# A hybrid attention and expert layer: the end of the output projection taken two outputs at a time, transposes on both sides of a broadcast, and small work moved between VectorE and GpSimd

## The chip, the cores and the metric

The kernel runs on one core of one Trainium2 chip. The metric is the device time of one execution in microseconds (us), the median of several executions. Beside it stands one profiled execution, whose span (first to last instruction on the core) is a little shorter than its own time. Engines are named as the profile names them: PE (TensorE matmuls), PEld (its weight loads), DVE (VectorE), ACT (ScalarE), POOL (GpSimd) and SP, which issues most transfers.

## The reference

One decoder layer on 256 tokens of width 1024, in float32, cut to what matters here:

```
mod = silu(c) @ w_ada + b_ada                 # split into sh1, sc1, g1, sh2, sc2, g2
h   = rmsnorm(x, norm1_g) * (1 + sc1) + sh1
q, k, v, u = split(h @ w_in)                  # 512 columns each
mixed = concat(attention(q, k, v), pooling(u)) @ w_out
x   = x + g1 * mixed
h2  = rmsnorm(x, norm2_g) * (1 + sc2) + sh2
s   = scores of (h2 @ peer_wq) against two sets of 128 sub-keys, top 16 of each, top 16 of the sums
x   = x + g2 * sum over chosen experts e of gate_e * gelu(peer_u[e] . h2) * peer_v[e]
out = rmsnorm(x, final_g)
```

There are 16384 experts. The kernel does not gather the chosen ones; it multiplies by all of `peer_u` and `peer_v`, with gates that are zero for experts that were not chosen.

## The kernel before, in words

The whole kernel is one program written out by hand: each engine runs its instructions in the order in which the code issues them, and waits where data or a buffer is missing. Activations lie transposed (channels on partitions, 256 tokens along the free axis). Large matmuls run on numbers split in two: `hi` is the rounded part (ACT copies it), `lo` the rest (DVE subtracts, L522), and three products hi*hi, hi*lo and lo*hi are summed in PSUM.

The stages, in order of time:

- **Start.** `x`, `c` and a table `band` are loaded. `score_bias(h)` makes the bias table of each of 8 heads from `band`: heads 0 to 4 by one DVE instruction each (L192), heads 5 to 7 by two POOL instructions each (L194, L195). DVE and ACT square `x` (L254, L256), DVE adds the squares up (L259), PE sums them over partitions (L262), and `rstd_rows` makes 1/rms: a square root on ACT, four small DVE instructions, two diagonal tiles `dg` (L230), and a matmul of `ones` with `dg` (L231) that spreads the row over all partitions. `keep_warm(n)` (L241) issues n matmuls of `ones` whose result nobody reads.
- **First projection** (L330, L335), eight blocks `k` of `w_in`. In each, DVE makes two columns of `mod` (`ada_step`, L201, a dot product of a `w_ada` block with silu(c)), the scaled rows `t` (L306), two `lo` tiles (L316) and `hl` (L318); ACT makes `hh` (L313) and two `whi` (L274).
- **Attention and pooling**, with `ada_steps` between: these columns (G1, then SC2 and SH2 by turns) are needed later. Then the **output projection** `out_proj(n)`: block n of `w_out` (L457), eight outputs `m` each, for n = 0 to 7 as the heads' results come.
- **Second norm.** After all of block 7, DVE adds the projection to `x` (L545), ACT squares (L548), PE sums (L550), then 16 transposes (`turn_rows`, L536) of the new `x`, which ACT copies to `x2nat` (`turn_back`, L540), then `rstd_rows` again, and the loop over `k` that makes `t` (L591), `h2h` (L592) and `h2l` (L606) and multiplies them with the first three tiles of `peer_wq` (`first`, L584).
- **Queries, then `peer_u`** (L567, L568, L571), 16 and 128 tiles; the first 16 write to the PSUM banks of `q_bank` and are copied out by ACT (L839).
- **`peer_v`** (L992), steps i = 0 to 127, twelve matmuls each. Tiles come through three `raw` buffers that SP fills in order. The last three tiles are taken early, at steps 40, 50 and 60. In this stage the last columns of `mod`, g2, are made too: for each block k a load by POOL (`tail_load`), a DVE dot product (`tail_dot`, L201) and a diagonal tile (L951), a matmul of `ones` with it (`tail_pe`, L956), and a copy by ACT (`tail_evac`, L961), so that g2 stands in a row on all partitions. The final norm follows.

Loads are queued in `Loads`: SP issues them strictly in the order in which they were added, each when a buffer of its kind is free (7 of kind `ada`, 8 of `big`, 3 of `raw`).

Of the kernel before, what the change touches and what calls it, by code (L numbers as in the profile page):

```python
# [87 lines left out]
def _body(ctx, tc, xT, c, w_ada, cols, w_in, pool_w, w_out, peer_wq, subkeys, peer_u, peer_v, final_g,  # L88
# [84 lines left out]
    early = {40 + 10 * j: NQ + 2 * NK - 3 + j for j in range(3)}  # L173
    order = list(range(NQ + 2 * NK - 3))
    for i, n in early.items():
        order.insert(order.index(NQ + NK + i + 1) + 1, n)
# [364 lines left out]

    for m in range(0, KD, 2):
        out_proj(7, (m, m + 1))
    for m in range(KD):
# [2 lines left out]
        sqk = prepb.tile([P, T], F32, name="t", bufs=4)
        nc.scalar.activation(sqk, x2[:, m, :], AF.Square)  # L548
        for tb in range(2):
            nc.tensor.matmul(ps2[:, tb:tb + 1], lhsT=sqk[:, tb * P:(tb + 1) * P], rhs=ones[:, 0:1],  # L550
                             start=(m == 0 and tb == 0), stop=(m == KD - 1), skip_group_check=True)
# [599 lines left out]
```

## Time and profile before

| | |
|---|---|
| median of 3 runs | 922.27 us (920.63 to 922.82) |
| the profiled execution's own time | 922.48 us |
| its span | 920.7 us |
| PE busy | 906.1 us, 98% of the span |
| DVE busy | 692.5 us, 75% |
| ACT busy | 456.0 us, 50% |
| POOL busy | 15.1 us, 2% |
| moved by DMA | 185.40 MB, mean 201 GB/s |

The profiled execution lies 0.2 us over the median. PE has work nearly all the time, so what a change can win is PE work that goes away, PE waits, and PE work that runs at a lower clock. Time at which PE has nothing to do lies before the first projection, around the second norm, and after the last matmul.

### The profile page before, as it was taken

What the parts mean: (1) busy time and instruction counts of PE and PEld (TensorE: products, weight loads), DVE (VectorE), ACT (ScalarE), POOL (GpSimd) and SP (SyncE); (2) the same over time, 40 slices, a digit from 0 to 9 for tenths busy, and PEclk for the clock granted to TensorE, in tenths of its full rate; (3) what the DMA queues carried; (4) which work ended last, traced back from release to release, by engine and by line L of the source; (5) the groups of instructions that cost most, each with busy time, mean ns of one, the idle gap of its engine ahead of it and who ended that gap; (6) DMA issues with size and microseconds to landing.
All of it is one profiled execution on the core that took longest, in us unless ns stands there. A gap on an engine that the chain in (4) does not pass through costs nothing.

```text
span 920.7 us, 15894 instructions
## 1 busy us (share of the span) xinstructions
PE 906.1 (98%) x6267; PEld 829.4 (90%) x6267; DVE 692.5 (75%) x1285; ACT 456.0 (50%) x656; POOL 15.1 (2%) x24
## 2 busy tenths in 40 slices
PE   8999999999999999999999999999999999999996
PEld 7987889999999999999999998888888888888885
DVE  7999769899989778888889866555556656666665
ACT  5456355545454555454444445444456554444542
POOL 3000000000000000000000000000000000000001
PEclk9999999999999999999999999999999999999999
DMA  9988644566555555545555555666776776666551
GB/s 342 408 326 298 262 131 152 158 186 190 194 184 184 161 165 169 172 161 164 171 167 165 161 179 184 191 198 190 222 246 219 249 231 220 210 213 219 185 180 47
DMA packets 52061, 185.40 MB, mean 201 GB/s; under 512 B 6033, under 2 KB 6545, under 8 KB 51986
## 3 DMA queue, kind: packets, MB, share of 16 engines
q1 hardware_dynamic: 50402, 179.12, 58.8%
q0 software_dynamic: 1440, 5.25, 1.9%
q8 instruction: 49, 0.80, 0.4%
q14 instruction: 26, 0.21, 0.1%
q10 hardware_dynamic: 144, 0.01, 0.0%
HBM read 183.31 MB, written 1.05 MB: 200 GB/s over the span
## 4 chain that ended last, share of the span: by engine, by line
PE 96%; DVE 2%; ACT 1%; DMA 1%; issue 0%; SPq 0%; DVEq 0%
PE psum L992 37%; PE psum L567 15%; PE psum L568 14%; PE psum L571 14%; PE psum L330 4%; PE psum L457 3%; PE psum L798 2%; PE psum L799 2%; PE psum L335 1%; PE psum L584 1%; PE psum L848 1%; DMA xt<-in_xT_dram 1%; PE psum L241 0%; PE psum L550 0%; PE psum L536 0%; DVE a L1033 0%
## 5 line engine op out<-in xcount | busy, mean ns | idle before, releaser
L522 DVE TENSOR_TENSOR lo<-raw,hi 128x1024 fp32r<-128x1024 f32 x269 | 328.6, 1223 | 201.3 <-ACT hi L517 194.6
L517 ACT ACTIVATE hi<-raw 128x1024 fp32r<-128x1024 f32 x269 | 285.2, 1060 | 314.0 <-PE psum L992 142.0
L567 PE MATMUL psum<-h,hi 128*128 128x256 f32 x1128 | 273.4, 283 | 0.4 <-ACT q L839 0.4
L568 PE MATMUL psum<-h,hi 128*128 128x256 f32 x1128 | 269.7, 280 | 0.0
L992 PE MATMUL psum<-hi,h 128*128 128x512 f32 x972 | 240.8, 389 | 0.0
L992 PEld LDWEIGHTS psum<-hi,h 128*128 128x128 f32 x972 | 181.6, 188 | 37.3 <-ACT hi L517 0.2
L567 PEld LDWEIGHTS psum<-h,hi 128*128 128x128 f32 x1128 | 213.1, 189 | 0.6 <-ACT q L839 0.6
L568 PEld LDWEIGHTS psum<-h,hi 128*128 128x128 f32 x1128 | 213.0, 189 | 0.0
L571 PE MATMUL psum<-h,lo 128*128 128x256 f32 x1128 | 154.5, 280 | 0.0
L571 PEld LDWEIGHTS psum<-h,lo 128*128 128x128 f32 x1128 | 141.7, 189 | 0.0
L992 PE MATMUL psum<-lo,h 128*128 128x512 f32 x486 | 130.3, 388 | 0.0
L992 PEld LDWEIGHTS psum<-lo,h 128*128 128x128 f32 x486 | 91.2, 188 | 18.8
L201 DVE SCALAR_TENSOR_TENSOR junk<-ada,silc 128x1025 f32<-128x1025 f32 x40 | 48.9, 1221 | 0.9 <-DMA ada<-in_w_ada_dram 0.6
L817 ACT ACTIVATE a<-psum 128x256 f32<-128x256 f32 (+22 forms) x54 | 16.7, 352 | 60.6 <-DVE a L814 57.9
L899 DVE TENSOR_TENSOR h<-a,h 128x1024 fp32r<-128x1024 f32 x31 | 37.8, 1218 | 0.0
L798 PE MATMUL psum<-ah,ohb 128*128 128x128 f16 x256 | 33.1, 220 | 0.0
L799 PE MATMUL psum<-al,ohb 128*128 128x128 f16 x256 | 32.7, 218 | 0.0
L895 ACT ACTIVATE h<-a 128x1024 fp32r<-128x1024 f32 x31 | 32.4, 1046 | 0.0
L457 PE MATMUL psum<-cat,big 128*128 128x256 f32 x128 | 28.9, 382 | 0.0
L457 PEld LDWEIGHTS psum<-cat,big 128*128 128x128 f32 x128 | 23.9, 190 | 3.9 <-issue 0.7
L814 DVE SCALAR_TENSOR_TENSOR a<-psum,a 128x768 f32<-128x768 f32 (+31 forms) x42 | 27.2, 667 | 0.0
L825 ACT ACTIVATE a<-psum 128x512 f32<-128x512 f32 (+30 forms) x59 | 26.4, 448 | 0.0
(221 smaller groups left out, 755.5 us busy)
## 6 DMA issues: line engine op xcount, KB each, us to landing
raw<-in_peer_u_dram SPq DMA_DIRECT2D x128, 512.0 KB, 3.6
raw<-in_peer_v_dram SPq DMA_DIRECT2D x128, 512.0 KB, 4.3
ada<-in_w_ada_dram SPq DMA_DIRECT2D x40, 512.5 KB, 8.2
big<-in_w_in_dram SPq DMA_DIRECT2D x16, 512.0 KB, 10.3
raw<-in_peer_wq_dram SPq DMA_DIRECT2D x16, 512.0 KB, 3.7
a<-in_w_ada_dram POOLq DMA_DIRECT2D x8, 512.5 KB, 5.3
big<-in_w_out_dram SPq DMA_DIRECT2D x8, 512.0 KB, 6.9
out_dram<-a SPq DMA_DIRECT2D x4, 256.0 KB, 2.2
```

What stands on the lines that cost most here:

```text
L201: nc.vector.scalar_tensor_tensor(jk, blk, 1.0, sil, op0=ALU.mult, op1=ALU.mult, accum_out=ada[:, v * 8 + k:v * 8 + k + 1])
L330: nc.tensor.matmul(banks[m // 2][:, m % 2, :], lhsT=a[:, cs], rhs=b, start=(st and n == 0 and m % 2 == 0), stop=(sp and n == 2), skip_grou ...
L457: nc.tensor.matmul(ob[m // 2][:, m % 2, :], lhsT=w[:, m * P:(m + 1) * P], rhs=cat[:, k, :], start=(n == 0 and m % 2 == 0), stop=(n == 7), ...
L517: nc.scalar.activation(hi, raw, AF.Copy)
L522: nc.vector.tensor_sub(lo, raw, hi.bitcast(F32))
L567: nc.tensor.matmul(o, lhsT=hi[:, cs], rhs=h2h[:, k, :], start=(k == 0), stop=False, skip_group_check=True)
L568: nc.tensor.matmul(o, lhsT=hi[:, cs], rhs=h2l[:, k, :], start=False, stop=False, skip_group_check=True)
L571: nc.tensor.matmul(o, lhsT=lo[:, cs], rhs=h2h[:, k, :], start=False, stop=(k == KD - 1), skip_group_check=True)
L798: nc.tensor.matmul(o[:, t, :], lhsT=b[:, pr, :, e], rhs=ah[:, pr, :, e], start=True, stop=False)
L799: nc.tensor.matmul(o[:, t, :], lhsT=b[:, pr, :, e], rhs=al[:, pr, :, e], start=False, stop=True)
L899: nc.vector.tensor_sub(lo, a, hi.bitcast(F32))
L992: nc.tensor.matmul(ycols(tb, cs) if o is None else o, lhsT=a[:, i % 4, tb * P:(tb + 1) * P], rhs=b[:, cs], start=st, stop=sp, skip_group_c ...
```

## The change

The parts, each with what it does:

- **Output projection.** Blocks 6 and 7 of `w_out` are taken together, two outputs at a time. After each pair, `x2_pair` updates two rows of `x` and squares them; the `sums` of a pair are issued one pair later, between matmuls of the projection. One `ada_step` (SC2 of block 7) moves between the second and the third pair, the last one (SH2 of block 7) from ahead of `rstd_rows` to behind it.
- **Transposes.** Eight go ahead of the matmul that spreads 1/rms, eight behind it.
- **Loads.** Three `w_out` blocks are queued ahead of all eight G1 blocks of `w_ada`, six of which stood ahead of them.
- **Start.** All score biases are made by DVE: heads 0 to 5 at the start, 6 and 7 in blocks 3 and 4 of the first projection. POOL makes none. The warm-up matmuls around `rstd_rows` become 4 and 3 (5 and 5 before). The formula of 1/rms changes, with as many instructions as before.
- **`q_bank`** goes through four PSUM banks, three before.
- **`peer_v` stage.** The last three tiles are loaded by POOL to a place of their own, at steps 14, 18 and 22, and split at steps 30, 34 and 38. The g2 columns are made every 7 steps (9 before); a DMA writes each column into a row on one partition, and at step 108 one POOL instruction, `partition_broadcast`, copies the row to all partitions. The eight diagonal tiles, matmuls and copies go.

```diff
@@
-    for k, n in zip((4, 5, 6, 7, 0, 1, 2, 3, None), (6, 0, 0, 2, 2, 2, 2, 2, 8)):
+    for k, n in zip((4, 5, 6, 7, 0, 1, 2, 3, None), (0, 0, 0, 8, 2, 2, 2, 2, 8)):
         for _ in range(n):
             ada_load(*next(todo))
         if k is not None:
             load("big", ("wo", k), prep, [P, D], w_out[k], 8)
...
-    def score_bias(h):
-        b = biast[:, h, P:384]
-        if h < 5:
-            nc.vector.scalar_tensor_tensor(b, bandt[:, 0, :], -slopes[h], bandt[:, 1, :], op0=ALU.mult, op1=ALU.subtract)
-        else:
-            nc.gpsimd.tensor_scalar(b, bandt[:, 0, :], -slopes[h], None, op0=ALU.mult)
-            nc.gpsimd.tensor_sub(b, b, bandt[:, 1, :])
+    def score_bias(hs):
+        for h in hs:
+            nc.vector.scalar_tensor_tensor(biast[:, h, P:384], bandt[:, 0, :], -slopes[h], bandt[:, 1, :],
+                                           op0=ALU.mult, op1=ALU.subtract)
...
-    keep_warm(5)
+    keep_warm(4)
     rstd_rows(banks[7][:, 0, 0:2], banks[6][:, 0, :])
-    keep_warm(5)
+    keep_warm(3)
...
     for k in range(KD):
+        if k in (3, 4):
+            score_bias(range(k + 3, k + 4))
...
-    for n in range(4, 7):
+    for n in range(4, 6):
         ada_steps(3)
         out_proj(n)
-    ada_steps(2)
+    ada_steps(4)
...
+    def x2_pair(m):
+        for n in (m, m + 1):
+            nc.vector.scalar_tensor_tensor(x2[:, n, :], ob[n // 2][:, n % 2, :], acol(G1, n), xt[:, n, :],
+                                           op0=ALU.mult, op1=ALU.add)
+            SQ[n] = prepb.tile([P, T], F32, name="t", bufs=4)
+            nc.scalar.activation(SQ[n], x2[:, n, :], AF.Square)
+
+    def sums(m):
+        for n in (m, m + 1):
+            for tb in range(2):
+                nc.tensor.matmul(ps2[:, tb:tb + 1], lhsT=SQ[n][:, tb * P:(tb + 1) * P], rhs=ones[:, 0:1],
+                                 start=(n == 0 and tb == 0), stop=(n == KD - 1), skip_group_check=True)
+
     for m in range(0, KD, 2):
-        out_proj(7, (m, m + 1))
-    for m in range(KD):
-        nc.vector.scalar_tensor_tensor(x2[:, m, :], ob[m // 2][:, m % 2, :], acol(G1, m), xt[:, m, :],
-                                       op0=ALU.mult, op1=ALU.add)
...
-        if m == 3:
-            split_hi(0, [prepb.tile([P, D], F32R, name=x, bufs=2) for x in ("hi", "lo")])
-    turn_rows(range(KD))
+        for n in (6, 7):
+            out_proj(n, (m, m + 1))
+        x2_pair(m)
+        if m >= 2:
+            sums(m - 2)
+        if m == 2:
+            ada_steps(1)
+        if m == 4:
+            split_hi(0, two())
+    sums(KD - 2)
     split_lo(0)
-    ada_steps(1)
+    turn_rows(range(4))
     rstd_rows(ps2[:, 0:2], psb)
+    turn_rows(range(4, KD))
     turn_back(0)
     turn_back(2)
-    split_hi(1, [prepb.tile([P, D], F32R, name=x, bufs=2) for x in ("hi", "lo")])
+    split_hi(1, two())
+    ada_steps(1)
...
-        return psum[:, 1 + n % 3, 0:T]
+        return psum[:, (1 + n) % 4, 0:T]
...
-        jk = f1_[:, 0:D + 1]
-        ada_dot(G2, k, blk_of(k), jk, silc2)
-        nc.vector.tensor_scalar(jk[:, 0:P], ident, acol(G2, k), None, op0=ALU.mult)
-
-    def tail_pe(k):
-        o = psum[:, 6 + k % 2, :]
-        TP[k] = o
-        nc.tensor.matmul(o[:, 0:P], lhsT=ones, rhs=f1_[:, 0:P], start=True, stop=True)
...
+    def tail_row(k):
+        nc.gpsimd.dma_start(g2row[:, k * P:(k + 1) * P], acol(G2, k))
+
+    def tail_spread():
+        nc.gpsimd.partition_broadcast(g2r, g2row)
+
+    def early_load(j):
+        ld.ready["raw", NQ + 2 * NK - 3 + j] = early_raw[j]
+        nc.gpsimd.dma_start(early_raw[j], peer_v[NK - 3 + j])
...
```

Where the instructions stand is read from the built programs. First PE around the second norm, before the change: `big_941` is the last block of `w_out`, `t_...` are the squares of one output each, `xt_77` is the new `x`, and `dg_1129` the diagonal tile of 1/rms.

```order
L457 MATMUL psum_134<-cat_743,big_941 128x256 x8
L550 MATMUL psum_134<-ones_67,t_1060 128x1 x2
L550 MATMUL psum_134<-ones_67,t_1065 128x1 x2
L550 MATMUL psum_134<-ones_67,t_1070 128x1 x2
L550 MATMUL psum_134<-ones_67,t_1075 128x1 x2
L550 MATMUL psum_134<-ones_67,t_1083 128x1 x2
L550 MATMUL psum_134<-ones_67,t_1088 128x1 x2
L550 MATMUL psum_134<-ones_67,t_1093 128x1 x2
L550 MATMUL psum_134<-ones_67,t_1098 128x1 x2
L536 MATMUL psum_134<-ident_66,xt_77 128x128 x16
L231 MATMUL psum_134<-dg_1129,ones_67 128x256
L584 MATMUL psum_134<-h2_71,hi_1079 128x256
```

The same place after it, from the sums of the second pair on (`big_921` and `big_935` are blocks 6 and 7 of `w_out`; L450 is the projection, L529 the transposes, L223 the matmul with `dg`):

```order
L550 MATMUL psum_134<-ones_67,t_1050 128x1 x2
L550 MATMUL psum_134<-ones_67,t_1053 128x1 x2
L450 MATMUL psum_134<-cat_737,big_921 128x256 x2
L450 MATMUL psum_134<-cat_737,big_935 128x256 x2
L550 MATMUL psum_134<-ones_67,t_1066 128x1 x2
L550 MATMUL psum_134<-ones_67,t_1069 128x1 x2
L550 MATMUL psum_134<-ones_67,t_1083 128x1 x2
L550 MATMUL psum_134<-ones_67,t_1086 128x1 x2
L529 MATMUL psum_134<-ident_66,xt_77 128x128 x8
L223 MATMUL psum_134<-dg_1114,ones_67 128x256
L529 MATMUL psum_134<-ident_66,xt_77 128x128 x8
L595 MATMUL psum_134<-h2_71,hi_1075 128x256
```

Eight of the sums stand behind the last of the projection now, sixteen before, and eight of the transposes have moved behind the matmul with `dg`.

Then DVE at the same place, before the change (`lo` is `split_lo(0)`; the dot products of L201 read SC2 and SH2 of block 7, `ada_1011` and `ada_1014`; `m` to `dg` is `rstd_rows`; the last row makes `t` of k = 0):

```order
L201 SCALAR_TENSOR_TENSOR junk_76,ada_64<-ada_1011,silc_75 128x1025
L212 SCALAR_TENSOR_TENSOR ada_64<-ada_64,colt_63 128x1
L545 SCALAR_TENSOR_TENSOR xt_77<-psum_134,ada_64,xt_77 128x256 x8
L522 TENSOR_TENSOR lo_1080<-raw_1016,hi_1079 128x1024
L201 SCALAR_TENSOR_TENSOR junk_76,ada_64<-ada_1014,silc_75 128x1025
L226 TENSOR_SCALAR m_1122<-psum_134 128x2
L218 RECIPROCAL m_1122<-m_1122 128x2
L219 SCALAR_TENSOR_TENSOR m_1122<-m_1122 128x2
L220 TENSOR_TENSOR m_1122<-m_1122 128x2
L221 SCALAR_TENSOR_TENSOR m_1122<-m_1122 128x2
L230 TENSOR_SCALAR dg_1129<-ident_66,m_1122 128x128 x2
L591 SCALAR_TENSOR_TENSOR t_1138<-xt_77,ada_64,psum_134 128x256
```

And after it, from the point behind the first four updates of `x`:

```order
L196 SCALAR_TENSOR_TENSOR junk_76,ada_64<-ada_1005,silc_75 128x1025
L207 SCALAR_TENSOR_TENSOR ada_64<-ada_64,colt_63 128x1
L542 SCALAR_TENSOR_TENSOR xt_77<-psum_134,ada_64,xt_77 128x256 x4
L515 TENSOR_TENSOR lo_1076<-raw_1010,hi_1075 128x1024
L213 TENSOR_SCALAR m_1107<-psum_134 128x2
L216 RECIPROCAL m_1107<-m_1107 128x2
L217 TENSOR_TENSOR m_1107<-m_1107,m_1107 128x2
L218 TENSOR_TENSOR m_1107<-m_1107 128x2
L219 RECIPROCAL m_1107<-m_1107 128x2
L222 TENSOR_SCALAR dg_1114<-ident_66,m_1107 128x128 x2
L196 SCALAR_TENSOR_TENSOR junk_76,ada_64<-ada_1008,silc_75 128x1025
L602 SCALAR_TENSOR_TENSOR t_1132<-xt_77,ada_64,psum_134 128x256
```

The dot product of SH2 has moved from ahead of `m` to between `dg` and `t`, and `lo` now follows the last updates of `x` with only `m` behind it.

Last POOL's queue, from the start's work on, before the change (`a0` is the large buffer whose first parts fall free in the `peer_v` stage):

```order
L195 TENSOR_TENSOR biast_78<-biast_78,bandt_79 128x256
L964 DMA a0_1264<-in_c_dram 128x1024
L946 DMA a0_1264<-in_w_ada_dram 128x1025 x3
L974 DMA a0_1264<-in_final_g_dram 128x1024
L946 DMA a0_1264<-in_w_ada_dram 128x1025 x5
L1045 TENSOR_TENSOR a0_1264<-a0_1264 128x512 x2
```

And its end after the change, from the load of the last g2 block on (L965 writes a column into the row, the second ISA row is the broadcast):

```order
L956 DMA a0_1258<-in_w_ada_dram 128x1025
L965 DMA a0_1258<-ada_64 1x128x1
L968 ISA
L968 ISA a0_1258<-a0_1258 128x1024
L1067 ISA
L1067 TENSOR_TENSOR a0_1258<-a0_1258 128x512 x2
```

POOL has no arithmetic at the start any more; it has small transfers and one broadcast in the `peer_v` stage instead.

## Rows read from the trace of the kernel before

**Rows 1.** The page's chain of work that ended last: shares of the span.

```profile
PE 96%; DVE 2%; ACT 1%; DMA 1%; issue 0%; SPq 0%; DVEq 0%
```

**Rows 2.** Waits of PE: who waited for whom, us in total, times, longest.

```profile
PE psum L262 <- DVE x2nat L259: 1.7, 1, 1.7
```

**Rows 3.** Timeline of DVE and POOL: start us, us, instruction, count.

```profile
7.41 1.22 DVE L254 TENSOR_TENSOR x2nat<-xt 128x512 f32<-128x512 f32 x1
8.55 3.27 DVE L259 TENSOR_TENSOR x2nat<-x2nat 128x256 f32<-128x256 f32 x6
62.56 0.68 DVE L379 TENSOR_TENSOR pool<-x2nat 128x504 f32<-128x504 f32 x1
...
6.86 1.22 POOL L195 TENSOR_TENSOR biast<-biast,bandt 128x256 f32<-128x256 f32 x1
9.42 0.78 POOL L195 TENSOR_TENSOR biast<-biast,bandt 128x256 f32<-128x256 f32 x1
```

**Rows 4.** The chain in order of time, start and first projection: start us, us.

```profile
16.12 2.13 PE psum L241 x10
18.25 1.62 PE psum L330 x12
...
41.09 1.42 PE psum L330 x12
```

**Rows 5.** Timeline of ACT, DVE and SP, first projection; idle before in brackets.

```profile
16.67 0.51 ACT L313 ACTIVATE hh<-t,ada 128x256 fp32r<-128x256 f32 x1 [1.31 <-DVE t L306]
38.94 0.51 ACT L313 ACTIVATE hh<-t,ada 128x256 fp32r<-128x256 f32 x1 [3.13 <-DVE t L306]
...
58.06 1.22 DVE L201 SCALAR_TENSOR_TENSOR junk<-ada,silc 128x1025 f32<-128x1025 f32 x1
60.16 1.22 DVE L379 TENSOR_TENSOR x2nat<-uT 128x1020 f32<-128x1020 f32 x1 [0.88 <-ACT uT L348]
...
43.78 10.31 SPq L122 DMA_DIRECT2D ada<-in_w_ada_dram  x6
```

**Rows 6.** One window, first projection: busy of PE, PEld, DVE, ACT, POOL; PEclk, DMA, GB/s.

```profile
18.50:58.00 39.50, 39.50 (x294) 37.63 (x294) 39.26 (x64) 17.66 (x23) 0.00 (x0) 1.00 1.03 404
```

**Rows 7.** The chain in order of time, second norm.

```profile
107.38 3.46 PE psum L550 x32
110.85 3.46 PE psum L536 x16
...
117.38 10.11 PE psum L584 x68
```

**Rows 8.** Timeline of DVE and ACT, second norm.

```profile
104.83 3.46 DVE L545 SCALAR_TENSOR_TENSOR xt<-psum,ada,xt 128x256 f32<-128x256 f32 x8 [1.93 <-PE psum L457]
110.88 0.16 DVE L226 TENSOR_SCALAR m<-psum 128x2 f32<-128x2 f32 x1 [0.31 <-PE psum L550]
112.10 0.48 DVE L230 TENSOR_SCALAR dg<-ident,m 128x128 f32<-128x128 f32 x2
114.78 0.48 DVE L591 SCALAR_TENSOR_TENSOR t<-xt,ada,psum 128x256 f32<-128x256 f32 x1 [2.20 <-PE psum L231]
...
115.30 0.51 ACT L592 ACTIVATE h<-t,ada 128x256 fp32r<-128x256 f32 x1 [1.06 <-DVE t L591]
```

**Rows 9.** Windows of 1 us, second norm (columns as in rows 6).

```profile
118.00:119.00 1.00, 1.00 (x5) 0.74 (x4) 1.00 (x3) 0.69 (x2) 0.00 (x0) 0.50 0.85 320
121.00:122.00 1.00, 1.00 (x10) 1.00 (x10) 1.00 (x4) 0.72 (x2) 0.00 (x0) 1.00 0.27 111
```

**Rows 10.** Timeline of PE: the fourth query tile begins.

```profile
127.95 0.38 PE L567 MATMUL psum<-h,hi 128*128 128x256 f32 x1 [0.36 <-ACT q L839]
```

**Rows 11.** The chain in order of time, `peer_v` stage: one of eight such pieces.

```profile
742.34 0.22 PE psum L956 x2
```

**Rows 12.** Timeline of DVE and PE, `peer_v` stage.

```profile
833.31 1.23 DVE L522 TENSOR_TENSOR lo<-raw,hi 128x1024 fp32r<-128x1024 f32 x1 [1.49 <-ACT hi L517]
...
834.74 1.07 PE L992 MATMUL psum<-lo,h 128*128 128x512 f32 x4
```

More of the change, by code (lines that the diff above doesn't have):

```diff
@@ L172, in _body @@
     LAST = 5
[L173 to L176, printed above, removed]
+    early = {30 + 4 * j: NQ + 2 * NK - 3 + j for j in range(3)}
+    order = range(NQ + 2 * NK - 3)
     for n in order:
@@ L226, in rstd_rows @@
         nc.vector.tensor_scalar(m[:, 0:2], ps, 1.0 / D, EPS, op0=ALU.mult, op1=ALU.add)
-        rsqrt(m[:, 2:4], m[:, 0:2], m[:, 4:6])
+        nc.scalar.activation(m[:, 2:4], m[:, 0:2], AF.Sqrt)
+        nc.vector.reciprocal(m[:, 4:6], m[:, 2:4])
+        nc.vector.tensor_mul(m[:, 4:6], m[:, 4:6], m[:, 0:2])
+        nc.vector.tensor_add(m[:, 4:6], m[:, 4:6], m[:, 2:4])
+        nc.vector.reciprocal(m[:, 2:4], m[:, 4:6])
         dg = prep.tile([P, 2, P], F32, name="dg", bufs=1)
         for tb in range(2):
-            nc.vector.tensor_scalar(dg[:, tb, :], ident, m[:, 2 + tb:3 + tb], None, op0=ALU.mult)
+            nc.vector.tensor_scalar(dg[:, tb, :], ident, m[:, 2 + tb:3 + tb], 2.0, op0=ALU.mult, op1=ALU.mult)
         nc.tensor.matmul(psb, lhsT=ones, rhs=dg.rearrange("p a t -> p (a t)"), start=True, stop=True)
@@ L249, in _body @@
     keep_warm(5)
-    for h in range(NH):
-        score_bias(h)
+    score_bias(range(0, 6))
     for n, (a, b) in enumerate(xch):
@@ L540, in turn_back, with two @@
         nc.scalar.activation(x2nat[:, :, m * P:(m + 2) * P], turned[m // 2].rearrange("p (a d) -> p a d", a=2), AF.Copy)
-    for m in range(0, KD, 2):
-        out_proj(7, (m, m + 1))
-    for m in range(KD):
-        nc.vector.scalar_tensor_tensor(x2[:, m, :], ob[m // 2][:, m % 2, :], acol(G1, m), xt[:, m, :],
-                                       op0=ALU.mult, op1=ALU.add)
[L547 to L551, printed above, removed]
-        if m == 3:
-            split_hi(0, [prepb.tile([P, D], F32R, name=x, bufs=2) for x in ("hi", "lo")])
-    turn_rows(range(KD))
+    def two():
+        return [prepb.tile([P, D], F32R, name=x, bufs=2) for x in ("hi", "lo")]
+    SQ = {}
+    def x2_pair(m):
[9 more added lines that the diff above has]
+                                 start=(n == 0 and tb == 0), stop=(n == KD - 1), skip_group_check=True)
+    for m in range(0, KD, 2):
+        for n in (6, 7):
[8 more added lines that the diff above has]
+    sums(KD - 2)
     split_lo(0)
-    ada_steps(1)
+    turn_rows(range(4))
     rstd_rows(ps2[:, 0:2], psb)
+    turn_rows(range(4, KD))
     turn_back(0)
     turn_back(2)
-    split_hi(1, [prepb.tile([P, D], F32R, name=x, bufs=2) for x in ("hi", "lo")])
+    split_hi(1, two())
+    ada_steps(1)
     def mm3(o, n, ks=range(KD)):
@@ L939, in _body @@
     fg2 = f3[:, 0:D]
-    TP = {}
     def blk_of(k):
@@ L948, in tail_dot, with split_early @@
     def tail_dot(k):
-        jk = f1_[:, 0:D + 1]
-        ada_dot(G2, k, blk_of(k), jk, silc2)
-        nc.vector.tensor_scalar(jk[:, 0:P], ident, acol(G2, k), None, op0=ALU.mult)
-    def tail_pe(k):
-        o = psum[:, 6 + k % 2, :]
-        TP[k] = o
-        nc.tensor.matmul(o[:, 0:P], lhsT=ones, rhs=f1_[:, 0:P], start=True, stop=True)
-    def tail_evac(k):
-        o = TP[k]
-        ks = slice(k * P, (k + 1) * P)
-        nc.scalar.activation(g2r[:, ks], o[:, 0:P], AF.Copy)
+        ada_dot(G2, k, blk_of(k), f1_[:, 0:D + 1], silc2)
+    g2row = f1_[0:1, D:2 * D]
+    def tail_row(k):
[5 more added lines that the diff above has]
+        nc.gpsimd.dma_start(early_raw[j], peer_v[NK - 3 + j])
+    def split_early(n, place):
+        raw = ld.get(("raw", n))
+        nc.scalar.activation(place[0], raw, AF.Copy)
+        nc.vector.tensor_sub(place[1], raw, place[0].bitcast(F32))
+        splits[n] = place
+    early_raw = [f0[:, j * D:(j + 1) * D] for j in (1, 2, 3)]
     def tail_start():
@@ L975, in _body @@
     at(80, lambda: nc.vector.tensor_scalar(fg2, fg2, 2.0, None, op0=ALU.mult))
+    for j in range(3):
+        at(14 + 4 * j, early_load, j)
     for k in range(KD):
-        b = 50 + 9 * k
+        b = 50 + 7 * k
         at(b, tail_load, k)
         at(b + 5, tail_dot, k)
-        at(b + 6, tail_pe, k)
-        at(b + 7, tail_evac, k)
+        at(b + 6, tail_row, k)
+    at(108, tail_spread)
     def ycols(tb, cs):
@@ L1007, in _body @@
         if i in early:
-            split(early[i], spare.pop(0))
+            split_early(early[i], spare.pop(0))
         if i // 4 + 1 < 32 and i % 4 in (0, 1):
```

6 lines of the change are left out of this document (removed).

## The prediction

> **What bounds the kernel now.** The page's chain comes first: 96% of it is PE [rows 1], so time is won where PE loses work or stops waiting. The list of PE's waits gives the longest, 1.7 us at the first norm's sums, which wait for DVE [rows 2]. The chain in order of time shows the next place: in the second norm PE is busy to 114.31 (110.85 + 3.46) [rows 7], then waits for ACT's `h`, ready at 115.81 [rows 8]. In the first projection PE and DVE are both full, 39.50 and 39.26 of 39.50 us, and DMA too, at 404 GB/s [rows 6]: whoever is late there stays late. In the queries and both expert stages PE hardly waits, and only its own work counts.
>
> **The start.** POOL's bias instructions go. While its `TENSOR_TENSOR` ran from 6.86, DVE's square of 128x512 took 1.22; a like instruction of 504 columns took 0.68 with POOL idle [rows 3]. That is 0.54 over. The six adds took 3.27, while eight instructions of their 128x256 shape took 3.46 later [rows 8], 0.43 each, so 2.6 for six: 0.69 over, with POOL's next one from 9.42 among them. Sum 1.23 us on the chain that PE's longest wait hangs on. If POOL were not the reason, nothing would come of it; I take 1.23, since the excess lies where POOL ran.
>
> The sixth bias costs DVE 0.43 ahead of the squares and is hidden: DVE stood idle there for the first piece of `x`. The warm-up matmul dropped ahead of `dg`'s matmul ran beside the chain of 1/rms and costs or gives nothing. Behind it PE ran five, 2.13 us, to 18.25 [rows 4], while `hh` was ready at 17.18 (16.67 + 0.51) [rows 5]. Two fewer give 2/5 of 2.13, 0.85 us. The first projection so starts 1.23 + 0.85 = 2.1 us sooner on PE, but only 1.23 on DVE.
>
> DVE then gets two biases more in blocks 3 and 4, 0.43 each, with no idle time to take them: it reaches the dot product of G1 at 58.06 - 1.23 + 0.86 = 57.7 and ends it at 58.9 (1.22 long); with its accumulator read some 59.0. The pooling sums behind it began at 60.16 because `uT` came late [rows 5]; `uT` now comes 2.1 sooner, so DVE decides: 59.0, **1.2 us sooner**. Attention follows from DVE's work, so 1.2 passes on. PE feels nothing earlier: block 4 began at 41.09 [rows 4] and its `hh` was ready at 39.45 [rows 5], 1.64 of room, of which 0.85 + 0.86 = 1.7 goes. Bounds: 0.1 if POOL is not the reason (DVE then ends its dot product at 59.28 + 0.86, where the sums began anyway), 2.1 if DVE's extra work found room.
>
> Of TensorE's clock: the warm-ups took 0.43 each (2.13 over five) for 128 columns, where the same matmul in the last stage takes 0.22 [rows 11]; they run at 1.2 GHz. The projection's first twelve matmuls took 1.62, a later twelve 1.42 [rows 4], so PE comes to 2.4 GHz just as it starts, after five us of warm-ups with little between. If that rise does not come sooner with the rest, PE loses up to half of the 2.1 us, and 1.05 stay, hardly under DVE's 1.2.
>
> **Loads.** Three `w_out` blocks (0.5 MB each) go ahead of G1, whose first block is issued at 43.78 and used at 58.06 [rows 5]. At 404 GB/s [rows 6] they cost it 3.9 us of 14; hidden. Cover gone, DVE would wait what is missing. SP's queue behind that is the same.
>
> **The second norm.** Projection work and sums are as many as before, so PE ends the last sum at 110.85 [rows 7] unless it waits. It does a little: eight sums (0.216 each) stand behind the last pair, which ends at 109.1; DVE updates two rows (0.43 each, some 110.0), ACT squares, the last sum ends near 110.95. `split_lo(0)`, 1.23 us [rows 12], now sits on DVE between these updates and `m`, so `m` starts at 111.2, 0.3 later than 110.88. From `m` to the end of `dg` it was 112.58 - 110.88 = 1.70 [rows 8], with as many instructions now: `dg` at 112.9. PE, with eight transposes done by 112.7, multiplies it at once; before it came to it at 114.31. That is 1.4 us, but SH2's dot product (1.22 and its read) now stands between `dg` and `t`, so `t` starts near 114.1 where it stood at 114.78: **0.7 us**. The other eight transposes end near 115.1, when `h` is ready, 0.7 before its 115.81. `w_out`'s pairs and moved squares therefore pay nothing themselves; they make room for the rest.
>
> The clock is the unknown. At 118 us the granted clock is 0.50, 1.2 GHz, with 5 matmuls in 1 us; at 121 it is 1.00 with 10 [rows 9], after PE had mostly waited from 114.7 to 117.4. PE waits less now. No fall would give back half of some 3 us, of which about half is waiting anyway, 0.8; a second such stretch inside the 68 matmuls [rows 7] costs 1.5. I take **0.2**. Bounds for the place: -0.8 to 1.5.
>
> **Four query banks.** The fourth tile waited 0.36 for ACT to empty the first bank [rows 10]; bank 0 has long been emptied: **0.4** with the semaphore's time.
>
> **The g2 row.** Eight matmuls go, 0.22 each [rows 11]: **1.8 us** of pure PE work. What replaces them runs on POOL and on transfers. The three early tiles bring the same two splits each as before, in other steps; `peer_v`'s stream gets shorter by them.
>
> The room on DVE: `lo` ends at 834.54 (833.31 + 1.23), and its matmuls follow those that start at 834.74 by one step of 2.72 us, at 837.46 [rows 12]: 2.9 us. For the broadcast there is no row. POOL's 128x256 instruction took 0.78 to 1.22 [rows 3], so 1024 columns take 3.1 to 4.9 at that pace. It may hold DVE for some of that, half by the 0.54 in 1.22, inside the 2.9. I take 0; the bound is 2.0 lost.
>
> **The sum.** 1.2 + 0.7 + 0.2 + 0.4 + 1.8 = 4.3. The profiled execution took 922.48, so 918.2; it lies 0.2 over the median of 922.27, so **918.0**.
>
> **Rivals.** *The early gain is lost:* DVE's long instructions are not POOL's doing. Speaking against it: they fall where POOL's `TENSOR_TENSOR` runs. The start gives 0.1, 919.1. Chance 0.15.
>
> *The clock falls in the middle of the query matmuls:* 1.7 less than the 0.2 taken, 919.7. Chance 0.08; PE is busier there than before, which speaks against it.
>
> *The second norm doesn't do what it says:* squares or `split_lo` hold `m` back by more than the transposes free, so that `t` starts where it did. The 0.3 at `m` and the dot product behind `dg` speak for it. No gain there: 918.9. Chance 0.09.
>
> *Slower: the broadcast blocks DVE.* Every `lo` reads two operands from SBUF, and if DVE stands still for B us, PE loses B - 2.9. The change is lost at B = 7.2 and slower by 0.3% from B = 10. At 12, 918.0 + 9.1 = 927.1. Only the 0.54 over says that POOL can hold DVE at all, and POOL's pace gives no more than 4.9. Chance 0.06.
>
> The Trainium skill, page "SBUF — State Buffer", section "Who interferes with whom", says that a DVE instruction with two SBUF inputs contends with a GpSimd instruction that reads SBUF, and that the later one is blocked until the other is over. The trace agrees in kind, not in size: 0.54 over, beside a POOL instruction of 1.22. By that rule the two overlaps at the start could have cost up to 1.22 + 0.78 = 2.0, the gain there would be up to 0.8 more, and the time 917.2. The same rule speaks against the change at the broadcast, which would hold every `lo` for its whole length.
>
> **How the numbers follow.** The forecast has the other 0.62, with a range of its own of 916.6 to 919.2. All gains at their upper ends (2.1 + 1.5 + 0.4 + 1.8 = 5.8) give 916.5, all at their lower (0.1 - 0.8 + 0.4 + 1.8 = 1.5) 920.8, and with the broadcast's 2.0 lost besides 922.8; 916.3 to 920.2 leaves out the slow rival and the corners, 2 in 10 at most. About 0.3%, 2.8 us, is what a measurement of this kernel can tell from no change: faster means under 919.5. That holds for all but a little of the forecast (0.57 of 0.62), for most of the early rival (0.10), a third of the clock rival and most of the third (0.11 together): 0.78. Slower takes 0.05 of the last rival; 0.17 are left for the same.
>
> **What would show it.** No POOL instruction at the start, the 128x512 square near 0.7, the six adds near 2.6. First projection 2 us sooner on PE, pooling sums near 59.0. `m` near 110.0, its matmul right behind `dg` with a short wait before it, `t` two us sooner on the clock of the trace (1.2 and 0.7). No wait at the fourth query tile. No piece of 0.22 between the twelves of `peer_v`. I am wrong if `lo` or PE stands idle around step 108, if DVE's instructions at the start keep their length, or if the clock is at 0.50 for longer than before between 108 and 126.

## The result and the profile after

The changed kernel takes 916.9 us (median of 20 executions, 914.2 to 921.8), the kernel before 922.18 (20 executions, 919.2 to 923.9): ratio 0.9946, 95% interval 0.9933 to 0.9958, so 3.9 to 6.2 us sooner. The profiled execution took 917.33, with a span of 915.4.

PE has less of the page's chain than in [rows 1], since DVE's subtractions at the start of the projection now stand in it; and PE's wait of [rows 2] for the first norm's sums is 0.3 us instead of 1.7:

```profile
PE 91%; DVE 6%; issue 1%; ACT 1%; DMA 1%; SPq 0%; DVEq 0%; ACTq 0%
```

```profile
PE psum L253 <- DVE x2nat L250: 0.3, 1, 0.3
```

The start first, where [rows 3] stand. The columns of the timeline are start us, us, instruction, count, and in brackets the idle time before it and what ended it. DVE:

```profile
3.63 2.10 DVE L189 SCALAR_TENSOR_TENSOR biast<-bandt 128x256 f32<-128x256 f32 x6 [2.63 <-DMA bandt<-in_band_dram]
6.40 1.56 DVE L245 TENSOR_TENSOR x2nat<-xt 128x768 f32<-128x768 f32 x2 [0.67 <-DMA xt<-in_xT_dram]
12.96 0.48 DVE L222 TENSOR_SCALAR dg<-ident,m 128x128 f32<-128x128 f32 x2
14.76 0.48 DVE L299 SCALAR_TENSOR_TENSOR t<-xt,ada,psum 128x256 f32<-128x256 f32 x1 [0.17 <-PE psum L223]
...
58.60 1.22 DVE L372 TENSOR_TENSOR x2nat<-uT 128x1020 f32<-128x1020 f32 x1
```

The six biases fit in front of `x` (DVE still idles 0.67 for it), and the pooling sums begin at 58.60 instead of 60.16 [rows 5]. On PE the projection's first matmul starts at 15.84, where it was 17.90. Then the lead is lost. Windows of 1 us behind the first output block's begin (columns as in [rows 6]; PEclk 0.50 is 1.2 GHz):

```profile
70.00:71.00 1.00, 1.00 (x4) 0.35 (x3) 1.00 (x3) 1.00 (x4) 0.00 (x0) 0.51 0.35 45
71.00:72.00 1.00, 1.00 (x3) 0.82 (x4) 0.93 (x7) 1.00 (x5) 0.00 (x0) 0.50 0.79 221
72.00:73.00 1.00, 1.00 (x3) 0.80 (x3) 1.00 (x3) 1.00 (x6) 0.00 (x0) 0.50 0.96 324
73.00:74.00 1.00, 1.00 (x5) 0.81 (x4) 0.96 (x3) 0.41 (x2) 0.00 (x0) 0.78 0.78 217
```

Three matmuls a microsecond where the kernel before has six, at 1.00:

```profile
72.00:73.00 1.00, 1.00 (x6) 0.90 (x6) 0.96 (x5) 1.00 (x4) 0.00 (x0) 1.00 0.70 82
```

The sixteen matmuls of that block take 5.02 us instead of 3.72, and 1.3 of the 1.56 is gone. In the second norm (DVE, for [rows 8]) every start is late by that:

```profile
112.65 0.48 DVE L222 TENSOR_SCALAR dg<-ident,m 128x128 f32<-128x128 f32 x2
113.05 1.22 DVE L196 SCALAR_TENSOR_TENSOR junk<-ada,silc 128x1025 f32<-128x1025 f32 x1
...
114.19 0.48 DVE L602 SCALAR_TENSOR_TENSOR t<-xt,ada,psum 128x256 f32<-128x256 f32 x1
```

`t` starts 0.6 sooner than 114.78, with the dot product right in front of it. The fourth query tile, in PE's timeline, begins without the wait of [rows 10], 0.7 sooner than 127.95:

```profile
127.24 0.28 PE L578 MATMUL psum<-h,hi 128*128 128x256 f32 x1
```

Only 0.7 us of the 5.3 are won by then. The chain in order of time shows the rest: `peer_v` begins at 558.88 (before: 562.43), 2.8 more, and its matmuls end at 900.19 in one unbroken piece, where those before ended at 905.72 (890.92 + 14.80) with the eight pieces of [rows 11] among them, 2.0 more. The last part, 15.2 us for 15.0, gives 0.2 back.

```profile
558.88 341.31 PE psum L1014 x1505
```

The broadcast ran beside it, and no DVE instruction grew by it; the timelines of POOL and DVE:

```profile
850.86 1.81 POOL L968 PARTITION_BROADCAST a<-a  x1 [5.53 <-issue]
...
850.28 1.23 DVE L515 TENSOR_TENSOR lo<-raw,hi 128x1024 fp32r<-128x1024 f32 x1 [1.49 <-ACT hi L510]
853.00 1.23 DVE L515 TENSOR_TENSOR lo<-raw,hi 128x1024 fp32r<-128x1024 f32 x1 [1.49 <-ACT hi L510]
```

The 2.8 was in no forecast and in no edit: between 128 and 559 both kernels run the same matmuls without a wait. Windows of 10 us of the kernel before (the count of PE's instructions is in brackets), and of the changed one:

```profile
250.00:260.00 10.00, 10.00 (x87) 10.00 (x86) 10.00 (x53) 5.50 (x9) 0.00 (x0) 1.00 0.53 169
540.00:550.00 10.00, 10.00 (x87) 10.00 (x86) 6.10 (x6) 4.16 (x6) 0.00 (x0) 1.00 0.49 164
```

```profile
250.00:260.00 10.00, 10.00 (x90) 10.00 (x89) 10.00 (x53) 5.25 (x9) 0.00 (x0) 1.00 0.60 174
290.00:300.00 10.00, 10.00 (x91) 9.96 (x90) 8.88 (x13) 5.05 (x8) 0.00 (x0) 1.00 0.66 212
540.00:550.00 10.00, 10.00 (x91) 10.00 (x90) 6.05 (x6) 4.39 (x7) 0.00 (x0) 1.00 0.62 205
```

Same matmuls, clock 1.00 in both, yet 87 or 91 in 10 us: a step of 118 ns or of 113 from one to the next. From 250 to 300 and from 540 to 559 the changed kernel had the shorter step, 4% of 69 us, 2.8. So this pair of profiles agrees with the forecast in its sum (5.3 for 4.3) with two large items in it that nobody forecast, one of each sign. The experiments had to say which of them belong to the change.

### The profile page after: what moved, and what is told of

Its sections match the earlier page's. It is cut to its first block, busy times and chain, and to the rows that moved or that the text cites. A ratio compares the mean times of both kernels' runs of the same rounds, so it can differ in the third digit from the quotient of the medians.

```text
span 915.4 us, 15844 instructions
## 1 busy us (share of the span) xinstructions
PE 901.2 (98%) x6245; PEld 822.8 (90%) x6245; DVE 688.7 (75%) x1280; ACT 455.2 (50%) x648; POOL 16.7 (2%) x30
## 4 chain that ended last, share of the span: by engine, by line
PE 91%; DVE 6%; issue 1%; ACT 1%; DMA 1%; SPq 0%; DVEq 0%; ACTq 0%
PE psum L1014 37%; PE psum L578 14%; PE psum L579 14%; PE psum L582 14%; PE psum L450 3%; PE psum L809 2%; PE psum L810 2%; DVE wlo L309 2%; DVE junk L196 1%; PE psum L595 1%; PE psum L859 1%; DMA xt<-in_xT_dram 1%; PE psum L323 0%; DVE hl L311 0%; PE psum L429 0%
## 5 line engine op out<-in xcount | busy, mean ns | idle before, releaser
L1014 PEld LDWEIGHTS psum<-lo,h 128*128 128x128 f32 x486 | 91.3, 188 | 18.7
L450 PE MATMUL psum<-cat,big 128*128 128x256 f32 x128 | 30.7, 395 | 0.0
L450 PEld LDWEIGHTS psum<-cat,big 128*128 128x128 f32 x128 | 24.7, 198 | 4.5 <-issue 1.2
```

Source lines behind the costliest of these rows:

```text
L450: nc.tensor.matmul(ob[m // 2][:, m % 2, :], lhsT=w[:, m * P:(m + 1) * P], rhs=cat[:, k, :], start=(n == 0 and m % 2 == 0), stop=(n == 7), ...
L1014: nc.tensor.matmul(ycols(tb, cs) if o is None else o, lhsT=a[:, i % 4, tb * P:(tb + 1) * P], rhs=b[:, cs], start=st, stop=sp, skip_group_c ...
```

## The experiments

The first three add one part of the change to the kernel before; the others start from the changed kernel. Each time is a median of 5 to 12 executions, measured in one of four groups beside 11 to 29 executions of the kernel before. Its median was 922.94 in the first group (the three parts and the filled gaps), 923.33 in the second (POOL back, the other orders, the eight broadcasts), 920.81 in the third (loads, banks, step) and 921.50 in the last. It moves by 2 us from group to group, so between groups 0.2% is not told apart, and 916.9 for the changed kernel belongs to none of the four. A gain in us is worked out from the ratio, which belongs to one group. Some edits are shortened to what they do.

**The start alone.** The `w_out` loads moved with it, as in the change.

```diff
-        if h < 5:  (DVE)  else:  (POOL, two instructions)
+        for h in hs:  (DVE, all eight; six here, one each in blocks 3 and 4)
-    keep_warm(5); rstd_rows(...); keep_warm(5)
+    keep_warm(4); rstd_rows(...); keep_warm(3)
```

> Before, with only the start of the change: all eight biases on DVE, two of them inside the projection, fewer filling matmuls around the first dg, w_out ahead of the ada blocks. Theory (POOL's TENSOR_TENSOR lengthened DVE's start): the 128x512 square near 0.7 us, six adds near 2.6, t(0) near 14.8 (before 16.16), the last pooling sum about 1.5 sooner than 60.16; how much of that stands at the end depends on whether a stretch at 1.2 GHz falls on the first output block, as it did in the changed kernel at 70.5 to 73.7: 922.2 less 0 to 1.4, so 920.8 to 922.2. Rival (nothing of POOL's doing): t(0) no sooner than 15.9, 922.2. Rival (all of it passes on in every execution): 920.8 with the clock at 1.00 from 58 to 92.

920.28, ratio 0.998 (0.9965 to 0.9995), 1.8 us sooner (0.002 of 922.94). `t` starts at 14.40, and at 70 to 74 the clock stayed: the output block's matmuls run through at six or seven a microsecond, and the fourth query tile comes 1.53 sooner than 127.95. PE's timeline:

```profile
70.25 3.51 PE L455 MATMUL psum<-cat,big 128*128 128x256 f32 x15
...
126.42 0.39 PE L565 MATMUL psum<-h,hi 128*128 128x256 f32 x1 [0.36 <-ACT q L837]
```

So the early gain passes on in full where no stretch at 1.2 GHz falls on it.

**The second norm alone.** The other formula of 1/rms came with it.

```diff
-    for m in range(0, KD, 2): out_proj(7, (m, m + 1))
-    for m in range(KD): ...x2, square, sums...
-    turn_rows(range(KD)); split_lo(0); ada_steps(1); rstd_rows(...)
+    for m in range(0, KD, 2): out_proj(6, ...); out_proj(7, ...); x2_pair(m); sums(m - 2)
+    sums(KD - 2); split_lo(0); turn_rows(range(4)); rstd_rows(...); turn_rows(range(4, KD))
-        return psum[:, 1 + n % 3, 0:T]
+        return psum[:, (1 + n) % 4, 0:T]
```

> Before, with only the second norm of the change: last two output blocks two outputs at a time with the sums between, turned rows halved around dg, the other order of the rstd arithmetic, four query banks. Theory (read from the changed kernel's trace): t(0) 0.6 sooner than before's 114.78, the fourth query tile without its 0.36 wait, about 0.55 sooner in all: 921.6. Rival (as predicted, 0.7 + 0.2 + 0.4): 920.9. Rival (m late by more than the halved rows save): 922.2 or slower.

919.48, ratio 0.9974 (0.9953 to 0.9996), 2.4 sooner. In the profile `t` starts at 114.08 and the fourth tile at 127.10, 0.7 and 0.85 sooner. The mean granted clock that each execution reports has a median of 0.995, against 0.992 for the kernel before in the same group; with the start alone it is 0.9925, with the tail alone 0.992. This part, then, is the one that takes stretches at 1.2 GHz away: its profile has one of them ahead of the last matmuls, at 117.7, where the kernel before has two, at 110.7 and 117.5. My theory had 0.55 us; the interval of the gain, 0.4 to 4.3, holds that as well.

**The tail alone.**

```diff
-        at(b + 6, tail_pe, k); at(b + 7, tail_evac, k)
+        at(b + 6, tail_row, k)     (and once, at 108: partition_broadcast)
+    for j in range(3): at(14 + 4 * j, early_load, j)
```

> Before, with only the tail of the change: the g2 row by eight small DMAs and one broadcast, the last three peer_v blocks loaded early on POOL's queue. Theory (the eight 0.22 pieces of L956 and nothing else): 1.8 sooner, 920.4, and the matmuls of the peer_u stage mixed between steps of about 113 and 118 ns as before. Rival (the 3 us more that the changed kernel won between 128 and 900 belong to the tail's edit): 917.4, with the quick step in most of that stage. Rival (the broadcast blocks DVE): slower than 922, with a DVE wait near the broadcast.

921.2, ratio 0.9977 (0.9962 to 0.9992), 2.1 sooner. The shorter step was not there: 118 ns from 180 to 300 and again from 540 to 560. The matmuls of `peer_v` take 341.7 us up to the end of their main row, where those before took 343.3: the tail's edit is worth its eight matmuls (1.6 of 1.8) and does not set the step.

**POOL back at the start.**

```diff
+    for h in (6, 7, 7):
+        b = biast[:, h, P:384]
+        nc.gpsimd.tensor_scalar(b, bandt[:, 0, :], -slopes[h], None, op0=ALU.mult)
+        nc.gpsimd.tensor_sub(b, b, bandt[:, 1, :])
```

> The changed kernel, with three TENSOR_SCALAR and three TENSOR_TENSOR of 128x256 put back on POOL at the start, on rows of biast that DVE writes again later; DVE's own work is unchanged. Theory (a POOL TENSOR_TENSOR beside DVE lengthens DVE's two-input instructions): DVE's 128x512 square and its six adds longer by 1.2 together, t(0) at 16.0 against 14.76, the last pooling sum as much later, 918.1 against 916.9. Rival (DVE's long start before came from its own order): t(0) stays at 14.8, 916.9.

918.24, ratio 0.9952 (0.9934 to 0.997), which the times do not tell apart from the changed kernel's 0.9946; the trace has to decide. DVE's own instructions are those of the changed kernel, and each group of them is longer (the biases 3.03 for 2.10, the squares 2.08 for 1.56, the adds 3.26 for 2.54); POOL's stand below:

```profile
3.80 3.03 DVE L189 SCALAR_TENSOR_TENSOR biast<-bandt 128x256 f32<-128x256 f32 x6 [2.80 <-DMA bandt<-in_band_dram]
6.75 2.08 DVE L249 TENSOR_TENSOR x2nat<-xt 128x768 f32<-128x768 f32 x2
8.76 3.26 DVE L254 TENSOR_TENSOR x2nat<-x2nat 128x256 f32<-128x256 f32 x6
...
16.36 0.48 DVE L303 SCALAR_TENSOR_TENSOR t<-xt,ada,psum 128x256 f32<-128x256 f32 x1 [0.17 <-PE psum L223]
```

```profile
7.08 1.20 POOL L246 TENSOR_TENSOR biast<-biast,bandt 128x256 f32<-128x256 f32 x1
9.63 0.78 POOL L246 TENSOR_TENSOR biast<-biast,bandt 128x256 f32<-128x256 f32 x1
```

The squares and adds are 1.24 over, as long as in the kernel before, and `t` starts 1.60 later than the changed kernel's 14.76: POOL was the cause. The delay lasts: the second norm's `m` starts at 111.38, where it starts at 109.65 in "three_banks" below; neither profile has a stretch at 1.2 GHz before it.

**Filling TensorE's gaps.** With matmuls of `ones` by `ones` into a bank that is free:

```diff
     s2(1)
+    keep_warm(2, 0)
     s3(0)
+    keep_warm(4, 0)
     turn_rows(range(4))
+    keep_warm(4, 3)
     rstd_rows(ps2[:, 0:2], psb)
     turn_rows(range(4, KD))
+    keep_warm(2, 3)
```

> The changed kernel, with 2 and 4 filling 128x128 matmuls in the two gaps of the attention's opening (0.62 and 1.05 us of waits) and 4 and 2 in the gaps around the second dg (0.87 and 0.51). Theory (the changed kernel gives its early gain back in a stretch at 1.2 GHz at 70.5 to 73.7, and another at 117.9 to 121.1, both behind gaps of TensorE): with the gaps filled neither stretch is there, 1.6 us each, 913.7 to 915.3 against 916.9. Rival (the clock falls for another reason, or in executions of its own choice): the stretches stay, 916.9. Rival (the filling matmuls stand in the way of the transposes and of h): slower by up to 0.8, 917.7.

916.0, ratio 0.9927 (0.9909 to 0.9945). At 70 to 74 the clock holds 1.00, and the mean clock is 0.996 or more in all six executions, which only 7 of the changed kernel's 20 reach. But the profile has a stretch elsewhere, at the second norm, where the four added matmuls, at 1.2 GHz, now hold PE:

```profile
110.94 1.92 PE L233 MATMUL psum<-ones 128*128 128x128 f32 x8
112.65 0.64 PE L223 MATMUL psum<-dg,ones 128*128 128x256 f32 x2
```

`dg` had been ready at 111.1. The fourth tile still comes at 125.43, 1.8 before the changed kernel's. The time misses my 913.7 to 915.3 and is not told apart from the changed kernel's.

**Another order, and both together.** The last dot product leaves its place behind `dg`, and `hi(2)` its place behind `h`; "best" has fillings besides (2 and 4 at the start of attention, 2 ahead of `dg`'s matmul):

```diff
-        if m == 2: ada_steps(1)
-        if m == 4: split_hi(0, two())
+        if m in (2, 4): ada_steps(1); split_hi(m // 2 - 1, two())
-    split_hi(1, two()); ada_steps(1)
+    split_hi(2)
```

> The changed kernel, with the last ada dot taken from between the second dg and t(0) to the gap of DVE behind the third pair of outputs, and the conversions hi(0), hi(1), hi(2) on ACT each one place sooner. Theory (the dot of 1.22 us holds t(0), and ACT's hi(2) holds the third query tile by 0.45): t(0) about 0.4 sooner behind dg, no wait for hi, the fourth query tile 0.8 sooner, 916.1 against 916.9. Rival (DVE, busy 1.00 from 114 on, is the limit whatever the order): the fourth query tile where it was, 916.9.

> The same reordering, with filling 128x128 matmuls in the attention's opening (2 and 4) and 2 ahead of the second dg's matmul. Theory (both work): no stretch at 1.2 GHz from 64 to 76, the fourth query tile at 124.5 or sooner, 915.0 against 916.0 for the kernel with fillings alone and 916.9 for the changed one. Rival (what one saves the other had saved already): 916.0.

916.28 (ratio 0.9928) and 915.36 (0.9917, 0.9892 to 0.9942). In the profile of "best" no stretch at 1.2 GHz is left ahead of the last 6 us. `t` follows `dg` by 0.8 instead of 1.06, and the fourth tile begins at 124.07. The wait for `hi` is gone but 0.9 of a wait for the second `h` has come in its place. DVE's timeline:

```profile
110.68 0.48 DVE L222 TENSOR_SCALAR dg<-ident,m 128x128 f32<-128x128 f32 x2
111.96 0.48 DVE L603 SCALAR_TENSOR_TENSOR t<-xt,ada,psum 128x256 f32<-128x256 f32 x1 [0.79 <-PE psum L223]
```

It beats the kernel before beyond doubt; against the changed one its 1.5 lies between two groups and is not settled.

**The broadcast eight times.**

```diff
+        for _ in range(8):
             nc.gpsimd.partition_broadcast(g2r, g2row)
```

> The changed kernel, with the broadcast of the g2 row issued eight times in a row. Theory (it costs DVE nothing): DVE's subtractions of 1.22 us beside it stay at 1.22, POOL is busy 14.5 us instead of 1.81, TensorE waits for nothing there, 916.9. Rival (DVE is held for the length of each broadcast that it meets): single subtractions of up to 3.0 us, more work than DVE's idle 40% can take, waits of TensorE for lo, 920 or more. By the Trainium skill (SBUF — State Buffer, Who interferes with whom) a VectorE instruction with two SBUF inputs contends with GpSimd's reads of SBUF; no run so far shows that for a broadcast.

915.89, no later. The timeline of POOL, which is busy without a break from 851.13 to 866.43, at the second, third and fourth broadcast, then DVE, whose instructions under them take up to 2.18 us instead of 1.23:

```profile
852.52 1.30 POOL L969 PARTITION_BROADCAST a<-a  x1
853.91 2.01 POOL L969 PARTITION_BROADCAST a<-a  x1
856.01 2.01 POOL L969 PARTITION_BROADCAST a<-a  x1
...
852.66 2.10 DVE L515 TENSOR_TENSOR lo<-raw,hi 128x1024 fp32r<-128x1024 f32 x1 [1.49 <-ACT hi L510]
855.38 1.48 DVE L515 TENSOR_TENSOR lo<-raw,hi 128x1024 fp32r<-128x1024 f32 x1 [0.62 <-ACT hi L510]
856.78 2.18 DVE L910 TENSOR_TENSOR h<-a,h 128x1024 fp32r<-128x1024 f32 x1
858.88 4.28 DVE L515 TENSOR_TENSOR lo<-raw,hi 128x1024 fp32r<-128x1024 f32 x2
863.54 1.72 DVE L515 TENSOR_TENSOR lo<-raw,hi 128x1024 fp32r<-128x1024 f32 x1 [0.38 <-ACT hi L510]
```

Six instructions are 4.4 over (11.76 for 6 x 1.23), and DVE's idle time pays it. The ends show that the two engines take turns. The subtraction of 852.66 starts under the broadcast that ends at 853.82 and ends 0.94 behind it, at 854.76; the next broadcast ends 1.16 behind that, at 855.92; the next subtraction 0.94 behind that, at 856.86; and so on to the last pair. My theory had the subtractions unchanged and was wrong. The rival had each of them held to the end of the broadcast that it meets, which is right, and its price wrong: a broadcast that nothing holds takes 1.30, and POOL is held in its turn. The Trainium skill (page "SBUF — State Buffer", section "Who interferes with whom") says that the later instruction is blocked until the other is over: the trace agrees, within 0.3 us (0.94 of a subtraction's 1.23 lies behind the broadcast). It agrees at the start of the kernel before as well: there the square starts at 7.41 [rows 3] under the instruction of POOL that ends at 8.08, and ends 0.55 behind it, its own 0.68 less 0.13. My "in kind, not in size" compared the 0.54 over with POOL's whole 1.22; the overlap was 0.67.

**Loads and banks.** In "loads_back" the six ada blocks stand ahead of `w_out`'s second block again, and the three `peer_v` tiles in SP's queue; "three_banks" has `1 + n % 3` again.

> The changed kernel, with the loads as before: six ada blocks again ahead of w_out's second block, and the last three peer_v blocks in SP's queue in their old places instead of early on POOL's. Theory (both are hidden): 916.9, TensorE waits for no load of w_out or peer_v. Rival (the loads hold a part of the gain): a wait of out_proj or of the last products for a load, or DVE's lo later, 918 or more.

> The changed kernel, with the query tiles in three banks of PSUM again. Theory (the fourth query tile waited for the copy of the first out of its bank): a wait of 0.36 to 0.45 of TensorE for ACT at the fourth query tile, 917.3 against 916.9. Rival (ACT, earlier now, has copied in time): no wait, 916.9.

916.92 and 916.35, where the kernel before had 920.81: neither is told apart from the changed kernel. In the first PE waits for no load of `w_out`, and in the expert stages once, 0.4 for a `hi`. In the second the wait is back, 0.36 at the fourth tile, which there begins at 125.89. That gives the size that times cannot: 0.4.

**The step.** Three transposes of the identity, as the retrieval's own three, at four steps:

```diff
         mm3(o, n)
+        if n in (24, 30, 36, 42):
+            for j in range(3):
+                nc.tensor.transpose(psum[:, 5, j * P:(j + 1) * P], ident, ident)
```

> The changed kernel, with three transposes of the identity, as the retrieval's three, put behind steps 24, 30, 36 and 42 of the peer_u stage (about 185 to 240 us), 0.9 us of added work. In every profile so far TensorE's matmuls of 128x256 stand 118 ns apart from 180 to 250, and behind the retrieval's transposes at 250 and 291 either 118 or 113 to 114. Theory (such a break lets the step be taken anew, whatever the place): stretches at 113 to 114 between 185 and 250 in the profile, up to 2.3 us sooner there, times from 2.3 less to 0.9 more, 916.2 in the middle. Rival (the step at 250 belongs to something else of that place): 118 throughout, 917.8.

917.44, between the theory's 916.2 and the rival's 917.8. In its profile the step stays at 118 ns behind the first break (196), goes to 113 behind the second (213), stays there behind the third and fourth, and is back at 118 behind the retrieval's own transposes at 250:

```profile
200.00:210.00 10.00, 10.00 (x87) 10.00 (x86) 9.04 (x40) 3.91 (x5) 0.00 (x0) 1.00 0.66 208
214.00:224.00 10.00, 10.00 (x91) 10.00 (x90) 9.42 (x45) 4.30 (x6) 0.00 (x0) 1.00 0.62 201
252.00:262.00 10.00, 10.00 (x88) 10.00 (x87) 9.39 (x46) 5.02 (x6) 0.00 (x0) 1.00 0.53 159
```

So each break lets the step be taken anew, and the one it takes varies: of the thirteen profiles of kernels with the retrieval's break at 250 as it was, seven took 113 there and six 118.

**The sums in one row.**

```diff
-        if m >= 2:
-            sums(m - 2)
-    sums(KD - 2)
+    for m in range(0, KD, 2):
+        sums(m)
```

> The changed kernel, with all sixteen one-column sums of the second norm in one row behind the last output again (eight tiles t instead of four for the squares); everything else as changed. The second norm itself should end where it did: m at 109.5 when the clock holds. Theory (in the kernel before, the clock fell behind the row of one-column sums at 107 to 111; spreading them between the projections is what took that stretch away, and is worth more than the 0.2 forecast): a stretch at 1.2 GHz between 108 and 115 in the profile, the mean granted clock of most runs back near 0.992 to 0.993 where the changed kernel has 0.995 to 0.996, 918.5 against 916.9. Rival (only gaps in which TensorE waits decide): no such stretch more often than before, mean clock 0.995 to 0.996, 916.9.

915.98, ratio 0.9941, mean clock 0.991 to 0.996. The stretch came where the theory put it, from 108.6 on, right behind the row of sums, but the time did not rise. `m` starts at 108.76, and PE's transposes at 1.2 GHz lie beside DVE's chain of 1/rms:

```profile
105.08 3.65 PE L550 MATMUL psum<-ones,t 128*128 128x1 f32 x32
108.59 1.95 PE L529 MATMUL psum<-ident,xt 128*128 128x128 f32 x8
110.52 1.22 PE L223 MATMUL psum<-dg,ones 128*128 128x256 f32 x2
```

The fourth tile begins at 123.89, before that of "best". My theory had the place of the stretch right and its price wrong. Nor are the spread sums what brings `m` forward: they hold it back (109.46 in "reorder", where the clock holds there too). With the stretch there, `t` follows `m` by 3.02 us (111.78), where it took 3.90 before: that is left for the halved transposes. This order together with that of "best" was not run.

## Why the prediction was right

**The start** (1.2, POOL's doing) held by its own steps: adds 2.54 for 2.6, PE's first projection matmul 2.06 sooner for 2.1, pooling sums at 58.60 for 59.0. POOL put back takes 1.6 at `t` and 1.7 at the second norm, and the start alone passes 1.53 on to the fourth tile. The sums came 0.4 sooner than worked out because `t` came 1.40 sooner (16.16 to 14.76), not 1.23, and a bias took 0.35 (six in 2.10), not 0.43.

**The second norm** (0.7), read where the clock held, is right: in "three_banks" `dg` stands at 110.88 and `t` at 112.42, which is 2.4 before 114.78 for the forecast's 1.9 (1.2 and 0.7). The fourth tile was to come 1.2 + 0.7 + 0.2 + 0.4 = 2.5 sooner, at 125.45; there it is 125.89 with the 0.36 wait in front, 125.5 without. "m near 110.0" was 109.65. With the start as before, in "norm_only", `t` is 0.70 sooner. But I did not see why PE came to `dg` as late as 114.31: in the kernel before the sixteen transposes lie in a stretch at 1.2 GHz, from 110.7 to 114.1.

```profile
112.00:113.00 1.00, 1.00 (x7) 1.00 (x6) 0.54 (x3) 0.74 (x2) 0.00 (x0) 0.50 0.12 45
```

Eight took 1.07 at full clock in the changed kernel; by that, an estimate, sixteen would have ended near 112.8, hardly behind `dg`. So the 0.7 is worth that much where the stretch falls on the transposes, and how much of it would be left without one no run shows.

**The clock** (0.2) is the term that was mis-sized, and mis-placed: I looked for stretches at 1.2 GHz in the second norm alone, and there only at 118. Between 108 and 126 the clock is down for 3.4 us (117.8 to 121.2) instead of 6.8, so my sign of being wrong did not come. In the profiled execution one fell at 70 and cost 1.3 of the start's gain; over all executions the mean granted clock rose from 0.992 to 0.995, and it rose with the norm's part. 0.003 of 920 us is up to 2.8 us, partly beside waits. That this is the way by which the norm's part alone gained 2.4 for a forecast of 1.3 is argued, not shown: its interval, 0.4 to 4.3, holds 1.3 as well.

**The banks** (0.4) and **the loads** (nothing) held as far as the runs can tell.

**The g2 row** (1.8) gave 2.0 in the profile and 2.1 alone. **The broadcast** cost nothing, as taken, though for a better reason than I gave: alone it takes 1.30, under the 3.1 to 4.9 from POOL's pace. In the changed kernel it was the later one, so it waited (it ended at 852.67, 1.16 behind the subtraction of 850.28) and held nothing. One that a subtraction meets adds 0.3 to 1.0 to it, inside the room of 2.9; the slower rival needed 10 us of hold.

The sum, 4.3, lies inside the measured 3.9 to 6.2. What the profiled pair shows above it came from the step (2.8 more) less the stretch at 70 (1.3 less): that this pair's 5.3 comes near 4.3 is in part luck. The three parts alone gave 1.8, 2.4 and 2.1, which is 6.3 with wide intervals. The steps of the parts, not the sum, show that the reasons were right.

## What to carry to other kernels

Compare two profiles stage by stage, and where a stage of equal work differs, look at the step from one matmul to the next before crediting an edit with it. Work on POOL is not free for DVE even when POOL is off the path: price it by DVE's own instructions beside it, which waited here for POOL's to end, and give it a place where DVE has idle time. A gain won ahead of TensorE's waits can be lost to the clock behind them, so a few filling matmuls there are worth a try, as few as still end before the real work when they run at 1.2 GHz.
